# Experts of a pair take turns by chunk: a mixture-of-experts stage on one Trainium2 core

## The chip, the cores and the metric

The program runs on one core of one Trainium2 chip. The core has five engines with instruction queues of their own: TensorE (PE in the profile, with PEld for its weight loads), VectorE (DVE), ScalarE (ACT), GpSimd (POOL) and SyncE (SP), which here issues nearly all transfers from memory. Every engine takes its instructions in the order that the build wrote down. The metric is the device time of one execution in microseconds (us); lower is better.

## The reference

Two transformer blocks of two layers each. The change touches one part, the routed feed-forward of the first block's second layer, on 256 tokens of width 1024:

```python
def moe_swiglu(h, w_router, b_router, w1, w3, w2):
    t = h.reshape(-1, shp[-1])                      # 256 x 1024
    logits = (t @ w_router) + b_router              # 8 experts
    top_v, top_i = lax.top_k(logits, 2)
    top_w = jax.nn.softmax(top_v, axis=-1)
    combine = jnp.sum(one_hot(top_i, 8) * top_w[..., None], axis=1)
    for e in range(8):
        ye = combine[:, e:e + 1] * swiglu(t, w1[e], w3[e], w2[e])
        y = ye if y is None else y + ye

def swiglu(t, w1, w3, w2):                          # inner width 2816
    return (jax.nn.silu(t @ w1) * (t @ w3)) @ w2
```

All weights are 4-byte floats. Expert by expert the reference multiplies all tokens; the kernel multiplies only the tokens that chose the expert.

## The kernel before, in words

The experts are sorted by how many tokens chose them and taken in pairs: experts 0, 2, 4, 6 of the program's count have 128 slots for tokens ("many" in what follows), experts 1, 3, 5, 7 have 64 ("few"). Each expert's weights come from memory in 33 pieces of 1 MB: 22 pieces of `exp_w13` (two make a chunk of 256 inner columns, so there are 11 chunks on the way up) and 11 pieces of `exp_w2` (the way down). SP issues the loads (lines 263 and 267) into a ring of seven `raw` tiles; a load waits until the tile it writes over has been used.

A **many** expert works in split form: every `raw` piece is cut in two halves of 128x1024, ScalarE casts a half into a high part (`hl<-raw`, line 290), VectorE subtracts it from the original for the low part (line 291), and TensorE makes three products from each 512 columns, always in the order of lines 306, 307, 308. Line 306 reads the high part, 307 the low part. Six such matmuls use up one half, so a chunk on the way up has four halves and 24 matmuls, a piece on the way down two halves and 12. High and low parts live in ten tiles named `hl`. After a chunk ScalarE takes the silu (line 1266), VectorE multiplies (1267), TensorE transposes (1270) and the two split the result again (311, 312).

A **few** expert uses the raw weights as they are. A chunk on the way up is 16 matmuls in the code, 32 in the trace (line 1250), then silu (1253), multiplication (1254), one transpose (1256) and a copy (1258). A piece on the way down is 4 matmuls in the code, 8 in the trace (line 1302).

Around them: `gather` (lines 1177 to 1183) collects the tokens of coming experts, `slots` code (1230 to 1237) makes each expert's combine weights, `scatter` (1194 to 1203) adds an expert's result to the tokens through VectorE (line 1203). In the loop over experts one whole expert stands behind the other; the scatter of an expert comes behind the third chunk of the next, the gather for the next two within the way down of a many expert. A branch in expert 2 (line 1290) guards a path for more than the slots hold, which these inputs do not take.

A scheduler at build time decides the order within each engine's queue out of the program's text and its own estimate of when things are ready; once built, the order is fixed. PSUM has eight banks: two `bkA` for the ways up, three `bkS` for the ways down, two `bkT` for transposes, gathers and scatters.

Of the kernel before, what the change touches and what calls it, by code (L numbers as in the profile page):

```python
# [10 lines left out]
F32 = mybir.dt.float32  # L11
F32R = mybir.dt.float32r
# [9 lines left out]
KC = 8  # L22
# [7 lines left out]
NPRE, R2, ISC, IGA = 3+int('42'[0]), (4, 2), 2, 3  # L30
# [168 lines left out]
def tile_kernel(ctx, tc, A, out, dbg=None, stop=None, mark=lambda s: None):  # L199
# [56 lines left out]
    def load(name, i, layer=None):  # L256
        offs, tot = piece_offsets(name)
        o, n, w = offs[i]
        src = A[name]
        raw = slot("raw", F32)  # L260
        if name.startswith("exp") and layer in expert_at:
# [788 lines left out]
    with phase("moe", 0, 3, 0) as mp:  # L1050
# [106 lines left out]
        def gather(es):  # L1157
# [3 lines left out]
            O = mp.tile([128, 2, 2, 128], F32R, name="O", bufs=1)  # L1161
# [9 lines left out]
            hg0 = mp.tile([128, 2, KC, 128], F32R, name="hg0", tag="hg0", bufs=1) if hi_ == 256 else None  # L1171
            hg1 = mp.tile([128, 2048], F32, name="hg1", tag="hg1", bufs=1) if lo_ == 64 else None
            for d in range(KC):
                p = bank("T")
                for v in range(2):
                    for t in range(2):
                        PE.matmul(p[:, v * 256 + lo_:v * 256 + hi_], htk[:, v, t, d * 128:(d + 1) * 128],
                                  O[:, t].rearrange("p j s -> p (j s)")[:, lo_:hi_], start=t == 0, stop=t == 1)
                if hg1 is not None:
                    V.tensor_reduce(hg1[:, d * 64:(d + 1) * 64], p.rearrange("p (v s) -> p s v", v=2)[:, 64:128, :],  # L1180
                                    axis=AX, op=ALU.add)
                for v in range(2 if hg0 is not None else 0):
                    last[0] = SC.copy(hg0[:, v, d, :], p[:, v * 256 + 128:(v + 1) * 256])
            return O, hg0, hg1

# [25 lines left out]
        last, made = [None], [None]  # L1211
        nx, back = gather((0,)), None
# [7 lines left out]
        for e in range(8):  # L1220
            mark(f"moe.{e}")
            few = e % 2 == 1
            j = 1 - e % 2
            O, hg0, hg1 = nx
            cw = cmb if e == 0 else order[:, 2]
            r = PLACES[e]

# [3 lines left out]
            ws = mp.tile([128, 1], F32, name="ws", bufs=2)  # L1231
# [4 lines left out]
            OT = mp.tile([128, S], F32R, name="OT", bufs=2)  # L1236
            SC.copy(OT, p[:, :S])
            GT = []
            for i in range(11):
                p = bank()  # L1240
                s = mp.tile([128, 256], F32, name="s", bufs=2)
                g = mp.tile([128, 256], F32, name="g", bufs=2)
                if few:

                    for k in range(2):
                        raw = whole("exp_w13", 2 * i + k, e)
                        for kc in range(4):
                            w4 = raw[:, kc * 512:(kc + 1) * 512].rearrange("p (m h c) -> p h m c", m=2, h=2)
                            for h in range(2):
                                PE.matmul(p[64 * h:64 * h + 64, :256].rearrange("p (m c) -> p m c", m=2),  # L1250
                                          hg1[:, (4 * k + kc) * 64:(4 * k + kc + 1) * 64], w4[:, h],
                                          start=k == 0 and kc == 0, stop=k == 1 and kc == 3)
                    SC.activation(s[:, :128], p[:, :128], AF.Silu)  # L1253
                    V.tensor_mul(g[:, :128], s[:, :128], p[:, 128:256])  # L1254
                    pt = bank("T")
                    PE.transpose(pt[:, :128], g[:, :128], ident)
                    gw = mp.tile([128, 256], F32, name="gw", tag="gh", bufs=12)
                    SC.copy(gw[:, :128], pt[:, :128])
                    GT.append(gw)
                else:  # L1260
                    for k in range(2):
                        wh, wl = piece("exp_w13", 2 * i + k, e)
                        for kc in range(4):
                            mm3t(p, hg0[:, 0, 4 * k + kc, :], hg0[:, 1, 4 * k + kc, :], wh[kc], wl[kc],
                                 k == 0 and kc == 0, k == 1 and kc == 3)
                    SC.activation(s, p[:, :256], AF.Silu)
                    V.tensor_mul(g, s, p[:, 256:])
                    pt = bank("T")
                    for c in range(2):
                        PE.transpose(pt[:, c * 128:(c + 1) * 128], g[:, c * 128:(c + 1) * 128], ident)  # L1270
                    gh_ = mp.tile([128, 256], F32R, name="gh", bufs=12)
                    gl_ = mp.tile([128, 256], F32R, name="gl", bufs=12)
                    hilo(gh_, gl_, pt[:, :256])
                    GT.append((gh_, gl_))
                if i == ISC and back:
                    scatter(*back)
                if i == 10 and e == 7:
                    early_table(s)
            yb = [bank("S") for _ in range(1 if few else 2)]
            for i in range(11):  # L1280
                if i == 0 and e == 0:
                    for v in range(1, 8):
                        expert_at[v] = nc.values_load(idx[0:1, PLACES[v]:PLACES[v] + 1], engines=[mybir.EngineType.SP],
                                                      min_val=0, max_val=7)
                if i == IGA and e == 2:

                    for k in range(i, i + NPRE):
                        prefetch("exp_w2", k, e)
                    nmax = nc.values_load(cmax[0:1, 0:1], min_val=0, max_val=256)
                    with tc.If(nmax > 128):  # L1290
                        with tc.For_i(0, 8, 1) as ev:
                            overflow(tc, mp, bank, A, ev, rank, sel8, cmb, cap, htk, accY, C, ident)
                if i == IGA and not few:
                    nx = gather((e + 1, e + 2) if e < 6 else (7,))
                if i == IGA and e == 7:
                    for c in range(KC):
                        given(c, accY[:, c, :])
                if few:
                    raw = whole("exp_w2", i, e)
                    for c in range(2):  # L1300
                        for q in range(2):
                            PE.matmul(yb[0][64 * q:64 * q + 64, :], GT[i][:, c * 64:(c + 1) * 64],  # L1302
                                      raw[:, c * 1024 + q * 512:c * 1024 + (q + 1) * 512],
                                      start=i == 0 and c == 0, stop=i == 10 and c == 1)
                    continue
# [6 lines left out]
            if few:  # L1312
                yh = mp.tile([128, D], F32, name="yw", tag="yh")
# [3 lines left out]
                back = (e, yh, None, OT)  # L1317
                continue
            yh = mp.tile([128, D], F32R, name="yh")
            yl = mp.tile([128, D], F32R, name="yl")  # L1320
            w = 512
            for q in range(0, D, w):
                sl, y = slice(q, q + w), yb[q // 512][:, q % 512:q % 512 + w]
                SC.activation(yh[:, sl], y, AF.Copy, scale=ws)
                V.scalar_tensor_tensor(yl[:, sl], y, ws, yh[:, sl].bitcast(F32), op0=ALU.mult, op1=ALU.subtract)
            back = (e, yh, yl, OT)
        scatter(*back)
# [458 lines left out]
def overflow(tc, mp, bank, A, ev, rank, sel8, cmb, cap, htk, accY, C, ident):  # L1786
# [18 lines left out]
    ws = tile_of("ws", (1,), 2)  # L1805
# [4 lines left out]
    OT = tile_of("OT", (S,), 2)  # L1810
# [95 lines left out]
```

## Time and profile before

| | us |
|---|---|
| median of 3 runs | 2396.64 (2389.97 to 2400.24) |
| the profiled execution, its own time | 2402.21 |
| its span from first to last instruction | 2400.3 |
| TensorE busy in the span | 2266.7 (94%) |
| VectorE busy | 1327.1 (55%) |
| ScalarE busy | 1099.8 (46%) |
| experts' stage, in the span | about 939 to 1690 |

Busy times of TensorE are modelled at an instruction's end and overlap their neighbours, so 94% is not 94% of its peak. The granted clock was 0.969 of full speed on average.

### The profile page before, as it was taken

The page shows a single profiled execution, that of the slowest core. Times are in us where ns is not written, and L with a number is a line of the kernel's source. Part 1 is how long each engine was busy: PE and PEld are TensorE (multiplying, and loading weights), DVE is VectorE, ACT ScalarE, POOL GpSimd, SP SyncE. Part 2 cuts the span into 40 slices and gives each one's busy share as a digit, 9 for nine tenths or more (in the row PEclk, how much of TensorE's full clock was granted, in tenths as well). Part 3 has the DMA queues.
Part 4 walks back from the last instruction along what each step waited for, and adds up shares of the span by engine and source line. Part 5 has one row for each costly group of instructions (what it writes and reads, how often), then busy time and mean ns, then how long its engine had stood idle before and what let it go on. Part 6 is the DMA issues. An engine that isn't in the chain of part 4 may idle for free. (4 is left out here: it accounts for less than half of the span.)

```text
span 2400.3 us, 35435 instructions
## 1 busy us (share of the span) xinstructions
PE 2266.7 (94%) x14070; PEld 1848.0 (77%) x14070; DVE 1327.1 (55%) x2365; ACT 1099.8 (46%) x1917; POOL 5.0 (0%) x12
## 2 busy tenths in 40 slices
PE   6999899999999999998998998998899999998997
PEld 4877678878879877764764774774698999898997
DVE  5655553333356556932841850861467775667665
ACT  4445642222245466732731750651345544465443
POOL 0000000000000000000000000000000000000000
PEclk9999899999999998999999999999899999999999
DMA  8141323233332445979979989989442555333542
GB/s 290 65 159 50 109 106 141 105 128 135 115 128 93 176 159 202 371 307 420 365 287 417 387 303 416 389 333 406 157 157 106 194 183 178 138 126 141 189 173 95
DMA packets 72838, 503.98 MB, mean 210 GB/s; under 512 B 8102, under 2 KB 10188, under 8 KB 14940
## 3 DMA queue, kind: packets, MB, share of 16 engines
q1 hardware_dynamic: 72012, 499.82, 55.0%
q8 instruction: 112, 1.84, 0.3%
q0 software_dynamic: 368, 1.43, 0.2%
q14 instruction: 58, 0.48, 0.1%
q10 hardware_dynamic: 288, 0.41, 0.1%
HBM read 500.58 MB, written 1.06 MB: 209 GB/s over the span
## 5 line engine op out<-in xcount | busy, mean ns | idle before, releaser
L291 DVE TENSOR_TENSOR hl<-raw,hl 128x1024 fp32r<-128x1024 f32 (+1 forms) x597 | 703.5, 1195 | 410.6 <-ACT hl L290 405.9
L290 ACT CAST hl<-raw 128x1024 fp32r<-128x1024 f32 (+1 forms) x597 | 602.2, 1026 | 428.2 <-PE bkS L302 153.3
L301 PE MATMUL bkA<-ph,hl 128*128 128x256 f32 x1080 | 309.7, 287 | 5.2 <-ACT ph L1448 4.5
L302 PE MATMUL bkA<-pl,hl 128*128 128x256 f32 x1080 | 307.5, 285 | 0.0
L303 PE MATMUL bkA<-ph,hl 128*128 128x256 f32 x1080 | 306.3, 284 | 0.0
L301 PEld LDWEIGHTS bkA<-ph,hl 128*128 128x128 f32 x1080 | 207.4, 192 | 7.8 <-ACT ph L1448 4.9
L302 PEld LDWEIGHTS bkA<-pl,hl 128*128 128x128 f32 x1080 | 207.7, 192 | 0.3
L303 PEld LDWEIGHTS bkA<-ph,hl 128*128 128x128 f32 x1080 | 207.5, 192 | 0.5 <-issue 0.3
L1250 PE MATMUL bkA<-raw,hg 128*64 128x256 f32 x1408 | 164.9, 383 | 0.0
L306 PE MATMUL bkA<-hl,hg 128*128 128x512 f32 x352 | 143.5, 408 | 5.3 <-ACT hl L290 5.1
L307 PE MATMUL bkA<-hl,hg 128*128 128x512 f32 x352 | 143.0, 406 | 3.0 <-DVE hl L291 2.3
L308 PE MATMUL bkA<-hl,hg 128*128 128x512 f32 x352 | 143.6, 408 | 0.0
L301 PE MATMUL bkA<-acth,hl 128*128 128x512 f32 (+1 forms) x376 | 138.4, 368 | 4.4 <-ACT acth L470 4.4
L303 PE MATMUL bkA<-acth,hl 128*128 128x512 f32 (+1 forms) x376 | 137.1, 365 | 0.0
L302 PE MATMUL bkA<-actl,hl 128*128 128x512 f32 (+1 forms) x376 | 136.8, 364 | 0.0
L1250 PEld LDWEIGHTS bkA<-raw,hg 128*64 128x64 f32 x1408 | 97.6, 137 | 50.8 <-issue 0.9
L301 PE MATMUL bkS<-acth,hl 128*128 128x512 f32 (+1 forms) x312 | 119.4, 384 | 2.8 <-ACT hl L290 2.8
L303 PE MATMUL bkS<-acth,hl 128*128 128x512 f32 (+1 forms) x312 | 119.0, 382 | 0.5 <-DVE hl L291 0.5
L302 PE MATMUL bkS<-actl,hl 128*128 128x512 f32 (+1 forms) x312 | 118.2, 379 | 0.0
L1254 DVE TENSOR_TENSOR g<-s,bkA 128x128 f32<-128x128 f32 x44 | 12.7, 289 | 173.1 <-ACT s L1253 173.1
L1302 PE MATMUL bkS<-raw,gw 128*64 128x512 f32 x352 | 79.9, 598 | 8.4 <-DMA raw<-in_exp_w_dram 8.4
L306 PEld LDWEIGHTS bkA<-hl,hg 128*128 128x128 f32 x352 | 67.6, 192 | 24.1 <-ACT hl L290 7.8
(528 smaller groups left out, 4276.1 us busy)
## 6 DMA issues: line engine op xcount, KB each, us to landing
raw<-in_exp_w_dram SPq DMA_DIRECT2D x264, 1024.0 KB, 7.6
raw<-in_w_mod_dram SPq DMA_DIRECT2D x48, 1024.0 KB, 5.0
raw<-in_w_up_dram SPq DMA_DIRECT2D x44, 1024.0 KB, 4.8
raw<-in_w_in_dram SPq DMA_DIRECT2D x32, 1024.0 KB, 4.8
raw<-in_ffn_w_dram SPq DMA_DIRECT2D x30, 1024.0 KB, 4.8
raw<-in_w_out_dram SPq DMA_DIRECT2D x16, 1024.0 KB, 4.8
raw<-in_w_down_dram SPq DMA_DIRECT2D x16, 1024.0 KB, 4.9
raw<-in_w_down_dram SPq DMA_DIRECT2D x8, 768.0 KB, 4.2
```

The costliest lines, as they stand in the source:

```text
L290: SC.copy(hi[:, :m], r)
L291: V.tensor_sub(lo[:, :m], r, hi[:, :m].bitcast(F32))
L301: PE.matmul(o, wh, xh, start=start, stop=False)
L302: PE.matmul(o, wh, xl, start=False, stop=False)
L303: PE.matmul(o, wl, xh, start=False, stop=stop)
L306: PE.matmul(o, th, wh, start=start, stop=False)
L307: PE.matmul(o, th, wl, start=False, stop=False)
L308: PE.matmul(o, tl, wh, start=False, stop=stop)
L1250: PE.matmul(p[64 * h:64 * h + 64, :256].rearrange("p (m c) -> p m c", m=2), hg1[:, (4 * k + kc) * 64:(4 * k + kc + 1) * 64], w4[:, h], sta ...
L1254: V.tensor_mul(g[:, :128], s[:, :128], p[:, 128:256])
L1302: PE.matmul(yb[0][64 * q:64 * q + 64, :], GT[i][:, c * 64:(c + 1) * 64], raw[:, c * 1024 + q * 512:c * 1024 + (q + 1) * 512], start=i == 0 ...
```

## The change

The two experts of a pair go through their weights together: chunk 0 of the many expert, chunk 0 of the few expert, chunk 1 of the many expert and so on, first on the way up, then on the way down. In the first pair the few expert follows three chunks late on the way up, in the last pair three pieces late on the way down. Both scatters of a pair come behind the fourth chunk of the next pair. The `hl` tiles go from ten to eight (`R2` from (4, 2) to (4, 0), which adds to three `raw` and eight `hl` of the base ring). The experts' numbers, which SP needs for the loads, are read pair by pair. New lines of the same operations: 1253/1254/1257 for the many expert's silu, multiplication and transpose, 1298 for the few expert's matmuls up, 1301/1302/1304/1306 for its silu, multiplication, transpose and copy, 1317 for its matmuls down, 1180 for the gather, 1197 to 1206 for the scatter.

```diff
-NPRE, R2, ISC, IGA = 3+int('42'[0]), (4, 2), 2, 3
+NPRE, R2, ISC, IGA = 7, (4, 0), 3, 3
...
-        for e in range(8):
-            few = e % 2 == 1
-            O, hg0, hg1 = nx
...
-            for i in range(11):
-                p = bank()
...
-                if i == ISC and back:
-                    scatter(*back)
-            yb = [bank("S") for _ in range(1 if few else 2)]
-            for i in range(11):
...
-                if i == IGA and not few:
-                    nx = gather((e + 1, e + 2) if e < 6 else (7,))
...
+        def many(e):
+            def up(i):
...
+                for k in range(2):
+                    wh, wl = piece("exp_w13", 2 * i + k, e)
+                    for kc in range(4):
+                        mm3t(p, hg[0][:, 0, 4 * k + kc, :], hg[0][:, 1, 4 * k + kc, :], wh[kc], wl[kc],
+                             k == 0 and kc == 0, k == 1 and kc == 3)
+                SC.activation(s, p[:, :256], AF.Silu)
+                V.tensor_mul(g, s, p[:, 256:])
...
+        def few(e):
+            def up(i):
...
+                SC.activation(s[:, :128], p[:, :128], AF.Silu)
+                V.tensor_mul(g[:, :128], s[:, :128], p[:, 128:256])
+                pt = bank("T")
+                PE.transpose(pt[:, :128], g[:, :128], ident)
+                gw = mp.tile([128, 128], F32, name="gw", bufs=11)
+                SC.copy(gw, pt[:, :128])
...
+        for pr in range(4):
+            ea, eb = 2 * pr, 2 * pr + 1
+            A_, B_ = many(ea), few(eb)
+            lag = 3 if pr == 0 else 0
+            if pr:
+                number(ea)
+                number(eb)
+            for i in range(11 + lag):
+                if i < 11:
+                    A_[0](i)
+                if i == 0 and pr == 0:
+                    gather((1,), O)
+                if i == 2 and pr == 0:
+                    number(eb)
+                if i >= lag:
+                    B_[0](i - lag)
+                if i == ISC:
+                    for b in back:
+                        scatter(*b)
+                    sa, sb = slots(ea), slots(eb)
+            lag = 3 if pr == 3 else 0
+            for i in range(11 + lag):
...
+                if i == IGA and pr < 3:
+                    O = gather((eb + 2, ea + 2))
+                if i < 11:
+                    A_[1](i)
+                if i == 10 and pr == 3:
+                    scatter(*A_[2](*sa))
...
+                if i >= lag:
+                    B_[1](i - lag)
+            back = [A_[2](*sa)] if pr < 3 else []
+            back.append(B_[2](*sb))
+        scatter(*back[0])
```

Two places of the fixed order show what moves. First ScalarE, on the way up in the second pair. Before, in the many expert 2 (`hl` casts with the number of the `raw` piece they read; `s` is the silu of a chunk, `gh` the split of its transposed result):

```order
L290 CAST hl_9540<-raw_9538 128x1024
L290 CAST hl_9544<-raw_9538 128x1024
L1266 ACTIVATE s_9480<-bkA_9479 128x256
L290 CAST hl_9562<-raw_9560 128x1024
L290 CAST hl_9566<-raw_9560 128x1024
L311 CAST gh_9531<-bkT_9528 128x256
L290 CAST hl_9596<-raw_9594 128x1024
L290 CAST hl_9600<-raw_9594 128x1024
L1266 ACTIVATE s_9536<-bkA_9535 128x256
```

Now, at the same place of the pair (L1253 is the silu of the many expert's chunk, L1301 that of the few expert's chunk, L1306 the few expert's copy):

```order
L1301 ACTIVATE s_9619<-bkA_9618 128x128
L290 CAST hl_9652<-raw_9650 128x1024
L1306 COPY gw_9645<-bkT_9643 128x128
L290 CAST hl_9656<-raw_9650 128x1024
L290 CAST hl_9674<-raw_9672 128x1024
L290 CAST hl_9678<-raw_9672 128x1024
L1253 ACTIVATE s_9648<-bkA_9647 128x256
L311 CAST gh_9699<-bkT_9696 128x256
L1301 ACTIVATE s_9704<-bkA_9703 128x128
L290 CAST hl_9737<-raw_9735 128x1024
```

Before, the casts of coming halves stood on both sides of a chunk's silu; pieces 9538 and 9560 belong to the chunk after the one whose silu stands between them. Now all four casts of the many expert's next chunk (pieces 9650 and 9672) stand behind the silu of the few expert's chunk that comes ahead of it.

Second TensorE in the same stretch: the last three of a many chunk's 24 matmuls, the few expert's chunk with the many expert's transposes in it (L1257) and its own behind it (L1304), and the first of the many expert's next chunk.

```order
L306 MATMUL bkA<-hl,hg_8674 128x512
L307 MATMUL bkA<-hl,hg_8674 128x512
L308 MATMUL bkA<-hl,hg_8674 128x512
L1298 MATMUL bkA<-raw,hg_8675 64x256 x5
L1257 MATMUL bkT<-cb,g 128x128 x2
L1298 MATMUL bkA<-raw,hg_8675 64x256 x11
L1304 MATMUL bkT<-cb,g 128x128
L306 MATMUL bkA<-hl,hg_8674 128x512
L307 MATMUL bkA<-hl,hg_8674 128x512
L308 MATMUL bkA<-hl,hg_8674 128x512
```

Before, TensorE in a few expert (here expert 1; L1256 is its transpose):

```order
L1256 MATMUL bkT<-cb,g 128x128
L1250 MATMUL bkA<-raw,hg_8336 64x256 x16
L1256 MATMUL bkT<-cb,g 128x128
L1250 MATMUL bkA<-raw,hg_8336 64x256 x16
L1256 MATMUL bkT<-cb,g 128x128
L1250 MATMUL bkA<-raw,hg_8336 64x256 x13
```

The few expert's transpose stands right behind its own last matmul in both; what follows it changed: the split matmuls of another expert, in place of the next chunk of its own.

## Rows read from the trace of the kernel before

**Rows 1.** The page: DMA by slices, the few expert's matmuls up, the experts' loads.

```profile
DMA  8141323233332445979979989989442555333542
...
L1250 PE MATMUL bkA<-raw,hg 128*64 128x256 f32 x1408 | 164.9, 383 | 0.0
...
raw<-in_exp_w_dram SPq DMA_DIRECT2D x264, 1024.0 KB, 7.6
```

**Rows 2.** Windows, all engines: us, busy (x instructions), clock, DMA share, GB/s.

```profile
939.00:1690.00 751.00, 699.73 (x3773) 478.69 (x3773) 390.81 (x523) 338.48 (x520) 0.00 (x0) 0.98 0.91 360
1160.00:1180.00 20.00, 20.00 (x92) 16.10 (x91) 17.42 (x21) 15.09 (x22) 0.00 (x0) 1.00 0.93 355
1300.00:1320.00 20.00, 15.22 (x64) 5.45 (x61) 3.95 (x4) 4.79 (x6) 0.00 (x0) 1.00 1.01 422
```

**Rows 3.** Waits of TensorE, 939 to 1690: total us, times, longest.

```profile
PE bkT L1256 <- DVE g L1254: 23.0, 40, 0.7
PE bkS L1302 <- DMA raw<-in_exp_w_dram: 8.4, 15, 0.7
PE bkT L1177 <- ACT hg L1183: 5.8, 9, 1.7
PE bkA L306 <- ACT hl L290: 5.1, 3, 1.7
PE bkA L307 <- DVE hl L291: 2.3, 3, 0.8
```

**Rows 4.** Timeline, a few expert's chunks: start, us, instruction, [idle before].

```profile
1271.54 0.28 ACT L1253 ACTIVATE s<-bkA 128x128 f32<-128x128 f32 x1 [3.35 <-PE bkA L1250]
...
1272.20 0.33 PE L1256 MATMUL bkT<-cb,g 128*128 128x128 f32 x1 [0.70 <-DVE g L1254]
1272.46 3.67 PE L1250 MATMUL bkA<-raw,hg 128*64 128x256 f32 x32
...
1276.83 0.33 PE L1256 MATMUL bkT<-cb,g 128*128 128x128 f32 x1 [0.70 <-DVE g L1254]
```

**Rows 5.** Timeline, from few expert 3 to many expert 4.

```profile
1312.42 1.94 PE L1302 MATMUL bkS<-raw,gw 128*64 128x512 f32 x8 [0.65 <-DMA raw<-in_exp_w_dram]
...
1314.40 0.69 ACT L1316 ACTIVATE yw<-bkS,ws 128x512 f32<-128x512 f32 x1 [21.90 <-PE bkS L1302]
1314.98 1.98 ACT L290 CAST hl<-raw 128x1024 fp32r<-128x1024 f32 x2
...
1316.07 0.49 PE L306 MATMUL bkA<-hl,hg 128*128 128x512 f32 x1 [1.71 <-ACT hl L290]
...
1317.33 0.50 PE L307 MATMUL bkA<-hl,hg 128*128 128x512 f32 x1 [0.77 <-DVE hl L291]
1317.66 0.39 PE L308 MATMUL bkA<-hl,hg 128*128 128x512 f32 x1
...
1319.77 0.40 PE L308 MATMUL bkA<-hl,hg 128*128 128x512 f32 x1
```

**Rows 6.** Timeline of TensorE, transposes within many expert 4.

```profile
1352.77 0.38 PE L1270 MATMUL bkT<-cb,g 128*128 128x128 f32 x2
...
1353.23 0.40 PE L307 MATMUL bkA<-hl,hg 128*128 128x512 f32 x1
```

**Rows 7.** Timeline of TensorE, way down of few expert 1.

```profile
1099.21 12.24 PE L1302 MATMUL bkS<-raw,gw 128*64 128x512 f32 x56
1111.78 1.94 PE L1302 MATMUL bkS<-raw,gw 128*64 128x512 f32 x8 [0.34 <-DMA raw<-in_exp_w_dram]
1114.29 1.94 PE L1302 MATMUL bkS<-raw,gw 128*64 128x512 f32 x8 [0.57 <-DMA raw<-in_exp_w_dram]
```

**Rows 8.** Groups by line, 939 to 1690: busy us, mean ns.

```profile
L291 DVE TENSOR_TENSOR hl<-raw,hl 128x1024 fp32r<-128x1024 f32 (+1 forms) x261 | 310.0, 1219 | 102.6 <-ACT hl L290 100.2 <-PE bkT L1177 0.2
...
L1203 DVE TENSOR_TENSOR xT<-xT,bkT 128x512 f32<-128x512 f32 x24 | 16.0, 686 | 7.7 <-PE bkT L1197 5.7 <-PE bkT L1194 1.9
```

**Rows 9.** Windows of 2 us: after a many expert's start, and in a gather.

```profile
1126.00:1128.00 2.00, 2.00 (x6) 1.57 (x5) 1.86 (x3) 1.50 (x3) 0.00 (x0) 0.50 1.01 422
...
1400.00:1402.00 2.00, 2.00 (x8) 1.58 (x8) 1.33 (x3) 0.87 (x4) 0.00 (x0) 0.50 0.90 340
```

More of the change, by code (lines that the diff above doesn't have):

```diff
@@ L1155, in tile_kernel, with gather @@
         nxt = adaln(S, idle=True)
-        def gather(es):
-            O = mp.tile([128, 2, 2, 128], F32R, name="O", bufs=1)
+        def gather(es, O=None):
+            if O is None:
+                O = mp.tile([128, 2, 2, 128], F32R, name="O", bufs=1)
             for e in es:
@@ L1178, in gather @@
                                   O[:, t].rearrange("p j s -> p (j s)")[:, lo_:hi_], start=t == 0, stop=t == 1)
-                if hg1 is not None:
-                    V.tensor_reduce(hg1[:, d * 64:(d + 1) * 64], p.rearrange("p (v s) -> p s v", v=2)[:, 64:128, :],
+                if lo_ == 64:
+                    V.tensor_reduce(hg[1][:, d * 64:(d + 1) * 64], p.rearrange("p (v s) -> p s v", v=2)[:, 64:128, :],
                                     axis=AX, op=ALU.add)
-                for v in range(2 if hg0 is not None else 0):
-                    last[0] = SC.copy(hg0[:, v, d, :], p[:, v * 256 + 128:(v + 1) * 256])
-            return O, hg0, hg1
+                for v in range(2 if hi_ == 256 else 0):
+                    last[0] = SC.copy(hg[0][:, v, d, :], p[:, v * 256 + 128:(v + 1) * 256])
+            return O
         def scatter(e, yh, yl, OT):
@@ L1209, in given @@
             V.scalar_tensor_tensor(xT[:, c, :S], y, mod[1][:, 40 + c, 0:1], xT[:, c, :S], op0=ALU.mult, op1=ALU.add)
-        last, made = [None], [None]
-        nx, back = gather((0,)), None
+        last, made, hg = [None], [None], [None, None]
+        O = gather((0,))
         with tc.issue_after(last[0].ins):
@@ L1242, in tile_kernel @@
                 g = mp.tile([128, 256], F32, name="g", bufs=2)
[L1243 to L1274, printed above, removed]
@@ new lines, in up @@
+                for k in range(2):
[6 more added lines that the diff above has]
+                pt = bank("T")
+                for c in range(2):
+                    PE.transpose(pt[:, c * 128:(c + 1) * 128], g[:, c * 128:(c + 1) * 128], ident)
@@ L1306, in tile_kernel, with down @@
+                gh_ = mp.tile([128, 256], F32R, name="gh", bufs=12)
+                gl_ = mp.tile([128, 256], F32R, name="gl", bufs=12)
+                hilo(gh_, gl_, pt[:, :256])
+                GT.append((gh_, gl_))
+            def down(i):
+                if i == 0:
+                    yb.extend(bank("S") for _ in range(2))
                 wh, wl = piece("exp_w2", i, e)
@@ L1311, in tile_kernel, with done @@
                              i == 0 and c == 0, i == 10 and c == 1)
-            if few:
-                yh = mp.tile([128, D], F32, name="yw", tag="yh")
+            def done(ws, OT):
+                yh = mp.tile([128, D], F32R, name="yh")
+                yl = mp.tile([128, D], F32R, name="yl")
+                for q in range(2):
+                    sl, y = slice(q * 512, (q + 1) * 512), yb[q]
+                    SC.activation(yh[:, sl], y, AF.Copy, scale=ws)
+                    V.scalar_tensor_tensor(yl[:, sl], y, ws, yh[:, sl].bitcast(F32), op0=ALU.mult, op1=ALU.subtract)
+                return e, yh, yl, OT
@@ new lines, in many, with down, done @@
+            return up, down, done
+        def few(e):
+            GT, yb = [], []
+            def up(i):
+                p = bank()
+                s = mp.tile([128, 256], F32, name="s", bufs=2)
+                g = mp.tile([128, 256], F32, name="g", bufs=2)
+                for k in range(2):
+                    raw = whole("exp_w13", 2 * i + k, e)
+                    for kc in range(4):
+                        w4 = raw[:, kc * 512:(kc + 1) * 512].rearrange("p (m h c) -> p h m c", m=2, h=2)
+                        for h in range(2):
+                            PE.matmul(p[64 * h:64 * h + 64, :256].rearrange("p (m c) -> p m c", m=2),
+                                      hg[1][:, (4 * k + kc) * 64:(4 * k + kc + 1) * 64], w4[:, h],
+                                      start=k == 0 and kc == 0, stop=k == 1 and kc == 3)
+                SC.activation(s[:, :128], p[:, :128], AF.Silu)
+                V.tensor_mul(g[:, :128], s[:, :128], p[:, 128:256])
+                pt = bank("T")
+                PE.transpose(pt[:, :128], g[:, :128], ident)
+                gw = mp.tile([128, 128], F32, name="gw", bufs=11)
+                SC.copy(gw, pt[:, :128])
+                GT.append(gw)
+                if e == 7 and i == 10:
+                    early_table(s)
+            def down(i):
+                if i == 0:
+                    yb.append(bank("S"))
+                raw = whole("exp_w2", i, e)
+                for c in range(2):
+                    for q in range(2):
+                        PE.matmul(yb[0][64 * q:64 * q + 64, :], GT[i][:, c * 64:(c + 1) * 64],
+                                  raw[:, c * 1024 + q * 512:c * 1024 + (q + 1) * 512],
+                                  start=i == 0 and c == 0, stop=i == 10 and c == 1)
+            def done(ws, OT):
+                yh = mp.tile([128, 512], F32, name="yw")
@@ L1326, in tile_kernel, with number @@
-            back = (e, yh, yl, OT)
-        scatter(*back)
+                return e, yh, None, OT
+            return up, down, done
+        def number(e):
+            expert_at[e] = nc.values_load(idx[0:1, PLACES[e]:PLACES[e] + 1], engines=[mybir.EngineType.SP],
+                                          min_val=0, max_val=7)
+        back = []
+        for pr in range(4):
+            mark(f"moe.{2 * pr}")
+            ea, eb = 2 * pr, 2 * pr + 1
[19 more added lines that the diff above has]
+            for i in range(11 + lag):
+                if i == IGA and pr == 1:
+                    for e in (ea, eb):
+                        for k in range(i, i + NPRE // 2):
+                            prefetch("exp_w2", k, e)
+                    nmax = nc.values_load(cmax[0:1, 0:1], min_val=0, max_val=256)
+                    with tc.If(nmax > 128):
+                        with tc.For_i(0, 8, 1) as ev:
+                            overflow(tc, mp, bank, A, ev, rank, sel8, cmb, cap, htk, accY, C, ident)
+                if i == IGA and pr < 3:
[4 more added lines that the diff above has]
+                    scatter(*A_[2](*sa))
+                    for c in range(KC):
+                        given(c, accY[:, c, :])
+                if i >= lag:
+                    B_[1](i - lag)
+            back = [A_[2](*sa)] if pr < 3 else []
+            back.append(B_[2](*sb))
```

57 lines of the change are left out of this document (13 added, 44 removed).

## The prediction, made before the changed kernel ran

> **What bounds the kernel now.** I began with the page's slices: from the sixteenth to the twenty-eighth the DMA share stands near its top, which it does nowhere else for long [rows 1]. That is the experts' stage. Its windows show two regimes [rows 2]. Within a many expert TensorE is busy without a break (20.00 of 20 us), VectorE nearly so (17.42), and the loads run at 355 GB/s. On a few expert's way down the loads run at 422 GB/s with a DMA share of 1.01, and TensorE waits. So the stage is bound by matmuls in one half and by loads in the other. All its weights, 264 pieces of 1.049 MB, would take 656 us at 422 GB/s; the stage takes 751. That difference invites the change.
>
> Then the waits of TensorE in the stage, which say what can be won [rows 3]: 23.0 us for VectorE's product ahead of the few expert's transposes, 8.4 us for loads, 5.8 us in gathers, 7.4 us at the three starts of a many expert.
>
> **What a chunk costs without waits.** Split matmuls follow each other by 0.234 us (nine steps from 1317.66 to 1319.77, [rows 5]), so 24 take 5.62; the two transposes add 0.23 (0.46 less one matmul, [rows 6]); together 5.85. The few expert's 32 rows follow each other by 0.106 ((3.67-0.38)/31, [rows 1, 4]), 3.40 us, and its transpose holds the next matmul up by 0.26: 3.66. A pair of chunks needs 9.51 us of TensorE. Its four loads need 9.94 at 422 GB/s. Before, the few chunk really takes 4.63 (1272.20 to 1276.83, [rows 4]), so the two chunks take 10.48.
>
> **The wait that the change adds.** In the fixed order the casts of the many expert's next chunk stand behind the silu of the few expert's chunk, and that silu waits for the few chunk's last matmul. Count from the modelled end of that matmul. Silu starts 0.04 later and takes 0.28 [rows 4]. The first cast starts 0.11 before the ScalarE instruction ahead of it ends, line 306 starts 1.09 after the cast's start, line 307 2.35 after it (1314.98, 1316.07, 1317.33, [rows 5]); there the instruction ahead is a `yw` of 0.69. With the silu in its place the cast starts at 0.21, line 306 at 1.30, line 307 at 2.56. Behind line 307 stand all the other matmuls of the chunk, since TensorE keeps its order. Without waits the transpose would have begun 0.27 before that end (0.38 less 0.106) and line 307 at 0.23 after it. So a full wait costs 2.33 us; the transpose's own wait of 0.70 lies inside it. From there on the halves come in time: TensorE needs six matmuls, 1.40 us, for each half, VectorE 1.22 [rows 8], ScalarE 0.99 [rows 5]. The pair of chunks then takes 11.84 us: more than its loads (9.94) and more than both chunks before (10.48). The bounds of this unseen wait: 0.97 (0.70 and 0.27) if cast and difference were ready and only the transpose had to wait, and 2.74 if the cast started as late as at a many expert's start, where line 307 comes 2.97 after the end. I take 2.33, since every link has a row and the order leaves no other.
>
> How often: counted in the order, all four casts stand behind the few expert's silu at 25 chunk ends (4 in the first pair, 7 in each other) and likewise ahead of the way down in pairs two and four: 27 times 2.33 is **+63 us**. Smaller ones: the ways down of pairs one and three, where a gather's matmuls cover some (1.6 each); three chunks with one cast ahead of the silu (1.2 each); three chunk ends ahead of a scatter and the last three few chunks of pair one, where the transpose's 0.70 and its 0.27 remain (0.97 each), and about 1.5 while pair one's few expert sets in: together **+13** (bounds 5 and 20).
>
> **The other terms.** The waits ahead of the few expert's transposes go, or lie inside the new one: 23.0 us, and 0.27 in each of 40 for the matmuls that could have followed: **-34**. The waits for loads on the few experts' ways down: a piece that waits comes 2.51 after the last (1111.78 to 1114.29), one that does not 1.72 ((12.24-1.94)/48 for a row, eight rows, [rows 7]); 15 times 0.79 is **-12**. They go because the way down alternates pieces of 2.81 and 1.72, 4.53 us for two loads of 4.97 together, and the seven `raw` tiles that the slow way up has filled make up the 11 times 0.44 that is lacking. The gathers' 5.8 us of waits [rows 3]: in two of the three large ones the order now puts ten split matmuls and a few expert's piece between their groups: **-4** (bounds -6 and 0). Both scatters fall in one chunk: VectorE has eight additions of 0.686 and four differences of 1.22 there [rows 8], 10.4 us against TensorE's 9.5 and the scatter's own matmuls, so banks may come back late: **+6** with the last pair's scatter within its way down (bounds 0 and 12). The starts of many experts 2, 4 and 6 keep their wait, behind a `yw` as before. SP's 264 loads and seven number reads stay as many; a slot is freed some 18 us before its next piece is needed, and a load lands 7.6 us after its issue [rows 1], so I price SP at nothing. That cover is gone only if the ways up became faster than the loads.
>
> **Clock.** After the wait at a many expert's start the granted clock was 0.50 of full, which is the lower level of 1.2 GHz, in 1126 to 1128, and likewise late in a gather with several short waits [rows 9]; after the same wait at 1317 the matmuls kept their 0.234 [rows 5], and after the single waits of 0.70 the rows of 3.67 too [rows 4]. A fall costs 0.6 us for each 2 us at 0.50 (six matmuls in place of 8.5); I take 1.2. The new waits leave TensorE a transpose and one matmul in 2.8 us, between the cases that fell and those that did not: one in four falls, 27/4 times 1.2 is **+8** (bounds 0 and 32).
>
> By the Trainium skill (TensorE: Matmul & The Clock Gate, the section on HAM oscillation) a loop that leaves TensorE idle long enough in every round begins every round at the lower level. By that rule the clock term would be 27 times 1.2, +32 in place of +8; the trace's own starts fell in some cases only.
>
> **Sum.** 63+13-34-12-4+6+8 = +40 on the profiled execution's 2402.2, so 2442; that execution lies 5.6 above the median of the runs, so **2437 us** beside 2396.64.
>
> **Rivals.**
> - *Faster, by the balance of loads and matmuls.* At one chunk end per pair, behind the scatter, three casts stand ahead of the few expert's silu and its transpose stands ten matmuls into the next chunk, so neither wait arises. If TensorE and ScalarE got by at all ends as they can there, +63 and +13 would go and the rest stay: -44 with no fall of the clock, 2353. For it speaks that after a chunk all eight `hl` tiles are free while 3.7 us of few matmuls run. Against it stands the order at the other ends. It decides from a wait of about 0.85 us downward, where 27 waits no longer outweigh what goes. A rule for it is in the Trainium skill (Perfetto Trace Analysis, Identifying Performance Opportunities, Optimization Strategy): where the most contended engine changes over time, interleaving the regimes may help. The windows do show such regimes; by the rule the time would be this rival's 2353. Chance 0.14.
> - *No change.* The waits sit at their lower bound of 0.97, because the next chunk's halves are ready and only the transpose's own wait stays: 26+13+6 meet the gains of 50, 2392. It needs the casts done within the few chunk's 3.7 us, which has the time for them but not the place in the order. Chance 0.15.
> - *The clock falls at nearly every wait.* +32 in place of +8: 2461, and 2472 with the wait at its upper bound (27 times 0.41 more). For it speak the starts that fell; against it, that a transpose and a matmul stand within the new wait, which those starts did not have both. Chance 0.14.
> - *My forecast*, 2415 to 2460. Chance 0.57.
>
> **Numbers.** About 0.5% (12 us) is what a measurement here tells from no change. Slower by more holds the forecast and the clock: 0.71; within it 0.15; faster 0.14. The range leaves out the faster rival (0.14) and what lies beyond the clock's upper end: 2390 to 2475.
>
> **What would show it.** In the trace after: between pieces of a pair's way up TensorE idle about 0.70 ahead of L1304, then some 0.3 ahead of L306 for ScalarE and 0.8 ahead of L307 for VectorE, 27 times, so that waits of L306 and L307 on the casts and differences rise from 7.4 us to some 40 or more; chunk pairs 11.8 us apart where casts stand behind, 9.5 where they do not; waits for loads at L1317 near zero; DMA below 400 GB/s on the ways up and the few 1.01 windows gone. Wrong would be: chunk pairs near 9.9 with TensorE waiting for loads (the balance), or L307 without a wait.

## The result and the profile after

The changed kernel takes 2484.2 us against 2396.6 before (medians of three executions each on one chip, with one disturbed execution of each kernel left out). The ratio of the means is 1.0376, interval 1.0336 to 1.0416: slower by some 88 us where 40 were forecast. The profiled execution has a span of 2486.8 us against 2400.3. All of the difference lies in the experts' stage. Counted in the timeline from the first matmul of a way up to the first of the way down behind it (before, both experts of a pair added), the four ways up take 599 us after 497, the four ways down 243 after 255.

From the page after, the lines that answer to [rows 1] (DMA share by slices; groups with busy us, mean ns, idle before; loads with KB and us to landing):

```profile
DMA  7232233333333366898888889888543455343542
L1298 PE MATMUL bkA<-raw,hg 128*64 128x256 f32 x1408 | 187.9, 385 | 0.0
L307 PE MATMUL bkA<-hl,hg 128*128 128x512 f32 x352 | 157.0, 446 | 24.0 <-DVE hl L291 24.0
L306 PE MATMUL bkA<-hl,hg 128*128 128x512 f32 x352 | 157.1, 446 | 12.4 <-ACT hl L290 12.2
```

From the seventeenth slice to the twenty-eighth the DMA share stood at 9 eight times; now it does twice. Lines 306 and 307 now wait. The waits of TensorE from 930 to 1780, which answer to [rows 3]:

```profile
PE bkT L1304 <- DVE g L1302: 24.1, 35, 0.7
PE bkA L307 <- DVE hl L291: 24.0, 33, 0.8
PE bkA L306 <- ACT hl L290: 12.2, 28, 1.7
PE bkS L306 <- ACT hl L290: 2.9, 3, 2.1
PE bkS L307 <- DVE hl L291: 2.2, 5, 0.6
```

The 23.0 us ahead of the few expert's transposes are still there under a new line number, the 8.4 us for loads are gone, and lines 306 and 307 wait 41.3 us in place of 7.4. Two chunk pairs from the timeline of TensorE:

```profile
1163.27 0.33 PE L1304 MATMUL bkT<-cb,g 128*128 128x128 f32 x1 [0.69 <-DVE g L1302]
1163.88 0.49 PE L306 MATMUL bkA<-hl,hg 128*128 128x512 f32 x1 [0.28 <-ACT hl L290]
1165.14 0.50 PE L307 MATMUL bkA<-hl,hg 128*128 128x512 f32 x1 [0.77 <-DVE hl L291]
...
1170.73 1.51 PE L1298 MATMUL bkA<-raw,hg 128*64 128x256 f32 x10
1172.17 0.44 PE L1257 MATMUL bkT<-cb,g 128*128 128x128 f32 x2
1172.53 2.80 PE L1298 MATMUL bkA<-raw,hg 128*64 128x256 f32 x22
1176.03 0.33 PE L1304 MATMUL bkT<-cb,g 128*128 128x128 f32 x1 [0.69 <-DVE g L1302]
1176.64 0.49 PE L306 MATMUL bkA<-hl,hg 128*128 128x512 f32 x1 [0.28 <-ACT hl L290]
...
1208.16 0.50 PE L306 MATMUL bkA<-hl,hg 128*128 128x512 f32 x1
...
1218.63 0.50 PE L306 MATMUL bkA<-hl,hg 128*128 128x512 f32 x1
```

From 1163.27 to 1176.03 is one chunk pair with the three waits, 12.76 us. At the two chunk starts behind the scatter, 1208.16 and 1218.63, no wait stands ahead of line 306: there casts stand ahead of the few expert's silu, and the pair between takes 10.47. So a full wait costs 2.29 us, and a pair without waits 10.47, not 9.51. What ScalarE does at the same chunk end:

```profile
1175.38 0.28 ACT L1301 ACTIVATE s<-bkA 128x128 f32<-128x128 f32 x1 [2.36 <-PE bkA L1298]
1175.55 1.04 ACT L290 CAST hl<-raw 128x1024 fp32r<-128x1024 f32 x1
...
1176.64 2.95 ACT L290 CAST hl<-raw 128x1024 fp32r<-128x1024 f32 x3
```

It is idle for 2.36 us with four casts to do, because the silu ahead of them waits for the few expert's last matmul. The third loss is the clock (windows; us, busy of PE, PEld, DVE, ACT and POOL, clock, DMA share, GB/s):

```profile
1151.00:1153.00 2.00, 2.00 (x5) 1.58 (x6) 2.00 (x3) 1.56 (x2) 0.00 (x0) 0.51 0.95 377
1165.00:1167.00 2.00, 1.86 (x8) 1.54 (x9) 2.00 (x3) 1.84 (x2) 0.00 (x0) 1.00 0.97 352
1148.00:1270.00 122.00, 110.29 (x569) 73.30 (x569) 54.95 (x69) 47.61 (x78) 0.00 (x0) 0.94 0.83 310
```

After the chunk end at 1149 the granted clock is 0.51, near the lower level of 1.2 GHz; after the equal one at 1163 it is 1.00. Pairs with such a fall last 14.2 to 14.3 us, those without 12.7 to 12.8: 1.53 each. In the timeline 25 chunk pairs begin with the full wait, and 16 of them have the fall too. Two ways down begin with a like wait (1.50 and 2.78 us of idle time), the second of them with a fall; three more falls follow the starts of many experts. Loads run at 310 GB/s, against 355 and 422 in [rows 2].

### The profile page after: what moved, and what is told of

It reads as the page before. It is cut to its first block, busy times and chain, and to the rows that moved or that the text cites. A ratio compares the mean times of both kernels' runs of the same rounds, so it can differ in the third digit from the quotient of the medians.

```text
span 2486.8 us, 35404 instructions
## 1 busy us (share of the span) xinstructions
PE 2336.0 (94%) x14070; PEld 1860.1 (75%) x14070; DVE 1331.8 (54%) x2365; ACT 1094.8 (44%) x1917; POOL 5.0 (0%) x12
## 5 line engine op out<-in xcount | busy, mean ns | idle before, releaser
L1298 PE MATMUL bkA<-raw,hg 128*64 128x256 f32 x1408 | 187.9, 385 | 0.0
L307 PE MATMUL bkA<-hl,hg 128*128 128x512 f32 x352 | 157.0, 446 | 24.0 <-DVE hl L291 24.0
L306 PE MATMUL bkA<-hl,hg 128*128 128x512 f32 x352 | 157.1, 446 | 12.4 <-ACT hl L290 12.2
L1298 PEld LDWEIGHTS bkA<-raw,hg 128*64 128x64 f32 x1408 | 104.1, 136 | 67.4 <-issue 21.9
L308 PE MATMUL bkA<-hl,hg 128*128 128x512 f32 x352 | 152.6, 434 | 0.0
L307 PEld LDWEIGHTS bkA<-hl,hg 128*128 128x128 f32 x352 | 74.4, 211 | 50.5 <-DVE hl L291 34.4
L306 PEld LDWEIGHTS bkA<-hl,hg 128*128 128x128 f32 x352 | 74.1, 210 | 40.2 <-ACT hl L290 20.0
L1253 ACT ACTIVATE s<-bkA 128x256 f32<-128x256 f32 x44 | 16.8, 383 | 173.7 <-PE bkA L308 173.7
```

The costliest lines, as they stand in the source:

```text
L306: PE.matmul(o, th, wh, start=start, stop=False)
L307: PE.matmul(o, th, wl, start=False, stop=False)
L308: PE.matmul(o, tl, wh, start=False, stop=stop)
```

## The experiments

The theory after the first look (theory A in the expectations): ScalarE's silu holds the casts up, 27 times; each fall of the clock adds 1.5 us; and each few chunk costs about 0.9 us more because something else stands in its row of matmuls. The rivals: slower loads set the pace and the waits only mirror them; the eight tiles; the alternation as such.

**Casts ahead of the silu.** ScalarE's order alone:

```diff
+                for n, j, v in soon:              # the two pieces of many's next chunk
+                    split[n, j, v] = piece(n, j, v)
+                with tc.issue_after(cast[0].ins) if soon else nullcontext():
                     SC.activation(s[:, :128], p[:, :128], AF.Silu)
```

> The changed kernel with one order altered: the casts of the many expert's next chunk stand ahead of the few expert's silu on ScalarE. Theory A (the 88 us are the waits behind that silu, about 63 us with the transpose's own, plus the clock falls that follow them, about 20, plus a cost at each change between the two kinds of matmul): the waits of lines 306 and 307 fall from 36 us to under 8, the few expert's transpose moves into the many expert's chunk and stops waiting, chunk pairs go from 12.76 (14.3 with a clock fall) to about 10.8, falls in the stage from 20 to under 10: 2390 to 2410 us. Theory B (the ways up are slow because the loads run slower there, and the waits only mirror them): TensorE waits for loads or casts elsewhere, 2465 to 2490 us.

Measured: 2403.5 us, 1.0032 (1.0015 to 1.0049). Its timeline:

```profile
1156.32 1.51 PE L1298 MATMUL bkA<-raw,hg 128*64 128x256 f32 x10
1157.76 0.44 PE L1257 MATMUL bkT<-cb,g 128*128 128x128 f32 x2
1158.13 2.80 PE L1298 MATMUL bkA<-raw,hg 128*64 128x256 f32 x22
1160.86 0.50 PE L306 MATMUL bkA<-hl,hg 128*128 128x512 f32 x1
```

The next chunk follows at once, pairs are 10.47 apart, and the clock falls only at three starts of pairs, in two scatter chunks and ahead of one way down. One order on ScalarE is worth some 81 of the 88 us, so loads did not set the pace. But it is no gain: a pair still costs 0.96 us more than forecast.

**Also the many expert's transposes behind the few expert's matmuls.**

```diff
                 V.tensor_mul(g, s, p[:, 256:])
+                return g                          # up() ends here; turn(g) comes later
+            def turn(g):
                 pt = bank("T")
                 for c in range(2):
                     PE.transpose(pt[:, c * 128:(c + 1) * 128], g[:, c * 128:(c + 1) * 128], ident)
```

> As the kernel before it in this set, and the many expert's two transposes stand behind the few expert's 16 matmuls and not among them, so that these are one run and not two of 10 and 22 rows. If cutting the run costs time (theory A counts about 0.45 us: the rows start in pairs 0.216 apart and each run ends with two single ones), 20 us less than with the casts alone, 2370 to 2390; if the cut costs nothing and the 0.115 to 0.144 us per row come from elsewhere (loads, clock), the same time as with the casts alone within 5 us.

Measured: 2488.9 us, 1.0377 (1.0335 to 1.042), some 100 us above what was expected. TensorE and ScalarE at one chunk end:

```profile
1142.72 3.67 PE L1301 MATMUL bkA<-raw,hg 128*64 128x256 f32 x32
1146.32 0.44 PE L1260 MATMUL bkT<-cb,g 128*128 128x128 f32 x2
1148.16 0.50 PE L306 MATMUL bkA<-hl,hg 128*128 128x512 f32 x1 [1.41 <-ACT hl L290]
1149.42 0.50 PE L307 MATMUL bkA<-hl,hg 128*128 128x512 f32 x1 [0.76 <-DVE hl L291]
```

```profile
1146.79 0.37 ACT L311 CAST gh<-bkT 128x256 fp32r<-128x256 f32 x1 [3.59 <-PE bkT L1260]
1147.06 3.88 ACT L290 CAST hl<-raw 128x1024 fp32r<-128x1024 f32 x4
```

The run is whole now (x32, 3.60 us to the transposes). But the cast of line 311, which reads these transposes, stands where the silu stood: ScalarE idles 3.59 us ahead of it, and the casts queue behind. It is the same loss by another instruction.

**And line 311 behind the casts too.**

```diff
                 if other:
-                    other()
+                    with tc.issue_after(cast[0].ins) if soon else nullcontext():
+                        other()                   # many's transposes and line 311
```

> As the version with the casts first and the many expert's transposes behind the few expert's matmuls, and now the cast that writes gh (line 311) too stands behind the four casts of the next chunk; in the earlier version it stood ahead of them and waited for those late transposes, so that line 306 waited 1.41 us and line 307 0.76 again. Theory A (whatever waits for a late TensorE result on ScalarE ahead of the casts costs the chunk end) expects those waits to go, and with the few expert's rows in one run (3.60 us to the next, against 1.44 and 2.73 in two) chunk pairs of about 10.0: 2375 to 2390 us. If only the silu mattered and the 2489 us came from the late transposes themselves, 2470 us or more.

Measured: 2375.4 us, 0.9905 (0.9875 to 0.9934): faster than both kernels, by 0.95% against the one before. In its timeline a pair lasts 9.69 us (1146.60 to 1156.29):

```profile
1146.60 0.44 PE L1260 MATMUL bkT<-cb,g 128*128 128x128 f32 x2
1146.79 0.47 PE L306 MATMUL bkA<-hl,hg 128*128 128x512 f32 x1
...
1152.69 3.67 PE L1301 MATMUL bkA<-raw,hg 128*64 128x256 f32 x32
1156.29 0.44 PE L1260 MATMUL bkT<-cb,g 128*128 128x128 f32 x2
```

So 0.78 of the 0.96 us came with the transposes in the middle of the few expert's run; 0.18 remain, about as much as the end of the run costs: from its first row to the transposes it is 3.60 us, where the forecast had 3.40.

**The cut alone, in the kernel before.** Two transposes of a constant in every few chunk: behind the fifth of its 16 matmuls (in two runs), behind the sixteenth, where TensorE waits anyway, and later behind the fourth:

```diff
+                                if (k, kc, h) == (0, 2, 0):      # the others: (1, 3, 1) and (0, 1, 1)
+                                    pd = bank("T")
+                                    for c in range(2):
+                                        with tc.issue_after(mm.ins):
+                                            mm = PE.transpose(pd[:, c * 128:(c + 1) * 128], ident, ident)
```

> The kernel before with one addition: in each of the few experts' 44 chunks two transposes of a constant (128x128, as the many expert's two, into a bank nobody reads) stand behind the fifth of the 16 matmuls, and the chunk's own transpose is held right behind its matmuls. If cutting the few expert's run is what costs (theory A), the chunk goes from 4.63 to about 5.55 us, as it did with the turns (5.30 from its first row to its transpose against 4.38), 40 us less up to 8 of waits for loads that then come in time: 2425 to 2440 us. If it is only the two transposes' own time (0.23 us for two among split matmuls), 2400 to 2410 us.

> The same addition, but the two transposes stand behind the sixteenth matmul, ahead of the chunk's own transpose, where TensorE waits 0.70 us for VectorE's product anyway: the same work without a cut. Both theories: 2390 to 2405 us, the chunk at 4.63.

> The kernel before with the same two transposes in each few chunk as in the cut kernel, but behind the fourth matmul and not the fifth. In the cut after the fifth the fifth and the last matmul's two rows start alone, one in a step of 0.216 us, where all others start two in a step (one matmul for each half of the 128 columns); that is two steps lost, 0.43 of the 0.93 us. If the pairing of the two column halves is it, an even cut costs 0.50 a chunk (the gaps around the transposes): chunks 5.13 apart, no single rows, 2413 to 2425 us. If any cut costs the same, 2425 to 2438 us and chunks 5.56 apart.

> The kernel cut behind the fifth matmul once more, on the chip of the even cut, so that the two stand side by side: 2425 to 2438 us, chunks 5.56 apart.

Measured: 2431.3 us, 1.0132 (1.0101 to 1.0164), and 2435.8, 1.0163 (1.0137 to 1.0189), behind the fifth; 2397.6, 1.0010 (0.9992 to 1.0028), behind the sixteenth; 2415.6, 1.0092 (1.0070 to 1.0113), behind the fourth. One chunk of each in the timeline, in the order fifth, sixteenth, fourth:

```profile
1278.36 1.51 PE L1250 MATMUL bkA<-raw,hg 128*64 128x256 f32 x10
1279.80 0.44 PE L1257 MATMUL bkT<-cb 128*128 128x128 f32 x2
1280.17 2.81 PE L1250 MATMUL bkA<-raw,hg 128*64 128x256 f32 x22
1283.66 0.33 PE L1262 MATMUL bkT<-cb,g 128*128 128x128 f32 x1 [0.69 <-DVE g L1259]
```

```profile
1276.00 3.67 PE L1250 MATMUL bkA<-raw,hg 128*64 128x256 f32 x32
1279.60 0.44 PE L1257 MATMUL bkT<-cb 128*128 128x128 f32 x2
1280.37 0.33 PE L1262 MATMUL bkT<-cb,g 128*128 128x128 f32 x1 [0.33 <-DVE g L1259]
```

```profile
1263.60 1.08 PE L1250 MATMUL bkA<-raw,hg 128*64 128x256 f32 x8
1264.62 0.44 PE L1257 MATMUL bkT<-cb 128*128 128x128 f32 x2
1264.99 2.81 PE L1250 MATMUL bkA<-raw,hg 128*64 128x256 f32 x24
1268.50 0.33 PE L1262 MATMUL bkT<-cb,g 128*128 128x128 f32 x1 [0.70 <-DVE g L1259]
```

From a run's first row to the chunk's transpose it is 5.30 us with the cut behind the fifth, just as with the turns, 4.37 without a cut, 4.90 behind the fourth. The same two transposes cost 0.93 us a chunk, nothing, and 0.53. The last section says why an odd cut costs more.

**The waits filled.** Matmuls of no use at the changed kernel's chunk ends; ScalarE's order is held, and only the chunk behind the scatter differs:

```diff
+                f = fill(2, mm) if i < 10 else None          # behind few's matmuls
...
+                    last[0] = fill(1, tr)                    # behind few's transpose
...
+                            f = fill(3, m0)                  # behind the first of line 306
```

> The changed kernel, in the same order, with matmuls of no use put into the waits at the chunk ends (two behind the few expert's matmuls, one behind its transpose, three behind the first of line 306, each 128x512 on data that is long there, into a bank nobody reads), so that TensorE has work in most of the 1.74 us and everything else still waits as long. Theory A (13 more clock falls at about 1.5 us each are 20 of the 88 us): falls in the stage from 20 to under 8 and 2462 to 2475 us. If the clock has no part, 2484 to 2495 us; if the casts and not TensorE decide the pace, no change either.

Measured: 2480.7 us, 1.0357 (1.0328 to 1.0386), less gain than expected. One chunk end and a window in the same columns as above:

```profile
1160.06 0.73 PE L1346 MATMUL bkS<-hg 128*128 128x512 f32 x2
1160.82 0.33 PE L1315 MATMUL bkT<-cb,g 128*128 128x128 f32 x1
1160.91 0.47 PE L1346 MATMUL bkS<-hg 128*128 128x512 f32 x1
1161.44 0.51 PE L1254 MATMUL bkA<-hl,hg 128*128 128x512 f32 x1
```

```profile
1148.00:1270.00 122.00, 119.99 (x633) 78.25 (x632) 55.07 (x71) 48.44 (x81) 0.00 (x0) 1.00 0.83 313
```

The clock is 1.00 where it was 0.94. Only two chunk pairs still have a fall, each the first of its pair of experts, which begins with a many expert's start and not with a filled wait; nearly all others that had the full wait stand at 12.75. That gives back the 1.53 us each. But the scatter's chunk, 17.2 to 17.8 us in the changed kernel, went up to 19.7 and 19.8 and the next from 10.47 to 12.34, which takes back about 4 us a pair, and the first pair, with matmuls of no use in chunks that had no full wait, became 4.3 longer. The falls cost what the pairs show; the sum of this kernel does not show it by itself.

**Two chunks a turn.**

```diff
-                if i >= lag:
-                    B_[0](i - lag)
+                if i >= lag and (i - lag) % 2:
+                    B_[0](i - lag - 1)
+                if i >= lag and ((i - lag) % 2 or i - lag == 10):
+                    B_[0](i - lag)
```

> The changed kernel with turns of two chunks: two of the many expert, then two of the few expert, so that there are five full turn ends in a pair and not ten on the way up. The casts of the next two chunks stand behind both silus and the copy behind the first transposes. Theory A: each turn end costs somewhat more (some 3.2 us and a clock fall) but there are half as many, 2425 to 2450 us. If the loss followed the bytes or the matmuls and not the number of turn ends, 2475 to 2495 us.

Measured: 2464.3 us, 1.0279 (1.0249 to 1.0309), between the two. Half as many turn ends do cost less, but two chunk pairs take 24.6 us, or 26.1 with a fall, or 27.0 to 27.1 with one that lasts longer, where two pairs without waits take 20.9. So a turn end costs 3.6 without a fall, where 3.2 were expected, and up to 6.2 with one. TensorE still waits 25.6 us ahead of line 1304.

**Turns on the way down only, eight tiles before, scatters apart.**

```diff
-                if i >= lag:
-                    B_[0](i - lag)
...
+            for i in range(11):
+                B_[0](i)
```

> Turns on the way down alone: on the way up the few expert's 11 chunks stand behind the many expert's 11, as before. From the two traces the four ways up took 102 us more after the change and the four ways down 12 us less. Theory A: only the gain of the ways down stays, 2380 to 2395 us. If the loss were one of the pair as a whole (eight hl tiles, both experts' numbers read together, both scatters in one chunk), 2410 us or more.

```diff
-NPRE, R2, ISC, IGA = 3+int('42'[0]), (4, 2), 2, 3
+NPRE, R2, ISC, IGA = 3+int('42'[0]), (4, 0), 2, 3
```

> The kernel before with eight hl tiles in place of ten and nothing else. Theory A gives the tiles no part: 2392 to 2404 us. If two tiles fewer hold the casts back by themselves, the half chunk that can no longer be ahead shows as waits of line 306 on the cast within many experts: 2410 us or more.

```diff
-                if i == ISC:
-                    for b in back:
-                        scatter(*b)
+                if i in (ISC, ISC + 3) and back:
+                    scatter(*back.pop(0))
+                if i == ISC + 3:
```

> As the kernel before it in this set, with the two scatters of a pair in two chunks (the fourth and the seventh) and the slots code with the second. With the casts first, the chunk that holds both scatters took about 20 us where others take 10.5, VectorE being late with eight additions and four differences. Theory A expects 5 to 15 us less than without this, 2362 to 2385; if the scatters cost their own TensorE time only, the same within 4 us.

Measured: turns on the way down only 2396.1 us, 0.9992 (0.9976 to 1.0008); eight tiles before 2396.7, 1.0002 (0.998 to 1.0024); scatters apart 2376.2, 0.9906 (0.9879 to 0.9934), the same as without. In the kernel before, two tiles fewer cost nothing; the changed kernel was not run with ten, but with the casts first its pairs run without these waits on the same eight. In the first of the three the ways down do gain 15 us, but the ways up take 13.5 more than before. The trace names most of it: some 6 us of gather matmuls (line 1180) stand in the ways up and no longer in the ways down; ahead of the four ways down line 306 waits 4.5 us for casts, behind the few expert's silu once more; and the few experts' transposes wait 27.6 us in place of some 23.7. Scatters apart: with both in one chunk it took 18.0 in place of 9.69, apart they take 11.7 and 16.0, the same 8.3 together. They cost that much wherever they stood; the 20 us that I expected to shorten held a fall of the clock (with the casts first 22.2 and 21.1 with one, 17.9 without).

## Why the prediction was wrong

The direction and the main mechanism were right; two terms were too small.

*The wait that the change adds* held in each link: 0.69, 0.28 and 0.77 ahead of lines 1304, 306 and 307, a full wait of 2.29 us for 2.33. There are 25 at chunk ends and two like them ahead of ways down, for 27 counted. Taken at 2.29 each, that is 62 us for 63. The few expert's transposes kept their own wait of 0.69; it lies inside the 2.29, as the forecast counted it. The first experiment shows it is the silu's place: with that changed, the waits go.

*What a chunk costs without waits* is the step that failed. It put 9.51 us; the pairs without waits take 10.47. Over 41 chunk pairs (11 in each pair of experts, 3 fewer in the first) that is 39 us for which the sum had nothing. The few expert's 32 rows were priced at 0.106 us, as they stand in one run in [rows 1, 4], and the transposes at 0.23, as they stand among split matmuls in [rows 6]. Yet the order that the front shows puts the two transposes in the middle of the few run. The kernel before with only this cut, behind the fifth matmul as there, loses 35 us; with the same transposes at the run's end nothing. In the changed order the run made whole gives back 0.78 of the 0.96 us.

*Clock* was mis-sized: 16 falls of 1.53 us in chunk pairs, 24 us, where 7 of 1.2 were put. The bounds (0 and 32) held it. The expectation that a transpose and one matmul within the wait keep most ends at the higher level was wrong; two equal ends, at 1149 and 1163, went either way. By the Trainium skill (TensorE: Matmul & The Clock Gate, HAM oscillation) a loop that idles long enough in each round starts each round at the lower level. Here 16 of the 25 chunk pairs behind a full wait did and nine did not; with the waits filled none of them did.

*The other terms*, -31 us in the forecast, are what remains: 86.5 less 39, 62 and 24 is -39. The waits for loads at line 1317 are gone as forecast. That the rest comes so near is in part luck, for it holds two things that the sum did not have. A pair of pieces on the way down takes 4.87 us and not 4.53:

```profile
1102.47 1.94 PE L1317 MATMUL bkS<-raw,gw 128*64 128x512 f32 x8
...
1107.34 1.94 PE L1317 MATMUL bkS<-raw,gw 128*64 128x512 f32 x8
```

If each of the 41 pairs of pieces costs so, that is some 14 us more. The other way, the clock no longer falls in the gathers: the three many experts' ways down with a gather in them stood at a granted clock of 0.92 before, the first three pairs' ways down stand at 1.00. In all the ways down gained 12 us, some 5 of them because gather matmuls that stood there now stand in the ways up. In the forecast's working the smaller waits add up to 14 and not 13, and the DMA share is near its top from the seventeenth slice on, not the sixteenth; neither decides anything.

*The rivals.* The faster one, by the balance, named the right lever: its condition (ScalarE gets by as it does behind the scatter) can be made by order, and then the time is 2403, or 2375 with the run uncut. It is not 2353, among other things since a pair of chunks takes 9.69 and not 9.51 and a pair of pieces 4.87 and not 4.53. The Trainium skill (Perfetto Trace Analysis, Identifying Performance Opportunities, Optimization Strategy) says that interleaving regimes may help. Here it does by 0.95%, but only once the order on ScalarE and TensorE fits. The rival with no change fell: the casts were not ready. The one with falls at nearly every wait was closest in time, 2461 to 2472, but by more falls than there were (27 for 16), and without the 39 us of a pair's own cost.

## What to carry to other kernels

When two streams of work alternate on one engine, look at what stands ahead of the next stream's preparation on the helper engines: an instruction that waits for the last result of this turn holds up all that is behind it, though its own work is 0.28 us. Price each instruction in the neighbourhood that the new order gives it, not in the one where the trace of before shows it. And a fix that moves one late instruction may put another in its place; read the helper's own timeline, where the idle time ahead of the first instruction names it.

## What the runs showed of the hardware

I had not expected that two small transposes within the few expert's matmuls could cost 0.93 us a chunk. Windows over single steps at the end of the changed kernel's run of 10 rows (us, busy, rows that run within, clock, DMA share, GB/s, of line 1298 alone):

```profile
1171.40:1171.60 0.20, 0.20 (x4) 1.00 1.35 573
1171.62:1171.82 0.20, 0.20 (x3) 1.00 1.17 492
1171.84:1172.04 0.20, 0.20 (x2) 1.00 0.42 164
```

A row (one record of a few expert's matmul in the trace) lasts 0.38 us, and a new step comes about every 0.22 (2.80 less 0.38 by eleven steps). Within a run two rows start in each step, so four are seen; in each of the last two steps only one starts. The code makes each product of a few expert in two matmuls, one for each half of the 128 columns (`h`), and the trace shows two rows for each matmul; a cut behind the fifth matmul leaves one of them without its partner, and the other side of the cut ends with one too. Two steps are lost, some 0.43 us. That the partners are the two halves is read from the code and these starts; the even cut bears it out, and no other run tests it. Behind the fourth matmul none is left alone: the chunk is 0.40 shorter, and the whole kernel 20 us. The other half of the 0.93 lies around the transposes: 0.31 us from the last row's start (1170.73 + 1.51 - 0.38) to the first of them and 0.36 from there to the next run, in place of one step.
